# A decoder layer whose gate and up products become one group, with seven quarter products for eight in two of the eight pairs of k-blocks

## The chip, the cores and the metric

One core of one Trainium2 chip runs the whole layer. The metric is the time of one execution on the device, in microseconds. Engines: TensorE (PE: the matmuls; its weight loads, PEld, overlap them), VectorE (DVE), ScalarE (ACT), GpSimd (POOL, all but unused here) and SyncE (SP), whose queue issues nearly all DMA.

## What is computed

All arrays are float32, batch 1, 256 tokens, width 2048, feed-forward width 5632:

```python
def swiglu_half_ffn(x, norm_g, w_gate_up, w_down):
    h = rmsnorm(x, norm_g)
    gate, up = jnp.split(h @ w_gate_up, 2, axis=-1)
    return 0.5 * ((jax.nn.silu(gate) * up) @ w_down)

x = x + swiglu_half_ffn(x, ffn1_norm, ffn1_w_gate_up, ffn1_w_down)
# token mixers: h @ w_in, causal pooling, 16-head attention with forget gates,
# 4-head attention over 256 memory tokens, three sigmoid gates, merged @ w_out
x = x + merged @ w_out
x = x + swiglu_half_ffn(x, ffn2_norm, ffn2_w_gate_up, ffn2_w_down)
```

Each `w_gate_up` is 2048 x 11264 (gate columns first, then up columns) and each `w_down` is 5632 x 2048. The change is in the two feed-forward halves; the mixers between them are only renamed onto other buffers.

## The kernel before

**One product.** TensorE multiplies in a rounded form of float32 (float32r), so each operand is split into a high part and a low remainder, and a product takes three matmuls: high x high, high x low, low x high. `mm_group` (L208) makes 256 tokens x 512 columns: for each k-block of 128 rows and each of the two token blocks t, three matmuls of 128x128 weights (the activations, "lhs") against 128x512 streamed columns of the weight matrix. It streams the matrix through three `raw` buffers of 1 MB (four k-blocks by 512 columns, one DMA on SP's queue, L217). Each half of a `raw` buffer is cut into `wh` (ACT, L228) and `wl` (DVE, L229), which have three buffers each, and 12 matmuls (L235) use it. After each such half, `tick()` emits one piece of side work from the queue `side`; that is how transposes, head norms and attention run beside the large products.

**One feed-forward half** (`ffn`, L271) goes over 11 blocks c of 512 columns. For each it makes the gate product, then the up product (two groups of 96 matmuls), SiLU on ACT (L283), gate times up on DVE (L289), and appends two side steps that transpose the result (L188, four transposes each) and split it (ACT L177, DVE L178) into `hid`, which stays in SBUF. Then four column groups of `w_down`, each with 44 k-blocks (264 matmuls), go to the callback `cb`, which adds them to the stream `xs` and queues the transposes for the next norm (`residual`, L254).

**Buffers.** Large SBUF tiles come from one pool of 15 slabs of 8 KB per partition. PSUM has 8 banks: four (`mp`) for products and four (`ap`) for transposes and attention. The Tile framework fixes each engine's instruction order at build time; an engine executes its own list in order, and waits are semaphores.

Of the kernel before, what the change touches and what calls it, by code (L numbers as in the profile page):

```python
# [31 lines left out]
def hybrid_layer(  # L32
# [30 lines left out]
    sp = ctx.enter_context(tc.tile_pool(name="sp", bufs=15))  # L63
# [3 lines left out]
    mp = ctx.enter_context(tc.tile_pool(name="mp", bufs=4, space=PSUM))  # L67
    ap = ctx.enter_context(tc.tile_pool(name="ap", bufs=4, space=PSUM))
# [14 lines left out]
    def slab(shape, dtype, name):  # L83
        return sp.tile([P, *shape], dtype, tag="s", name=name)
# [4 lines left out]
    def aux(shape, name):  # L89
        return ap.tile([P, *shape], F32, tag="a", name=name)  # L90

# [66 lines left out]
    def rsqrt(ss, n, scale, name):  # L158
        """(ss * scale + EPS) ** -0.5 by Newton's iteration."""
# [23 lines left out]
    def to_lhs_part(dst, jj, src, gains, name):  # L183
# [5 lines left out]
        if gains is None or isinstance(gains, float):  # L189
            split(dst, 2 * jj, 2, ps, gains)  # L190
        else:
            for j in range(2):
                k = 2 * jj + j
                split(dst, k, 1, ps[:, j : j + 1, :], gains[:, k : k + 1])

    def to_lhs(tiles, src, gains, name):
        """Two steps that append [P, 4, 2, S], the parts of the transposes of src(t) [P tokens, 512], to tiles."""

        def first():
            tiles.append(slab([4, 2, S], F32R, name))  # L200
            to_lhs_part(tiles[-1], 0, src, gains, name)

        return [first, lambda: to_lhs_part(tiles[-1], 1, src, gains, name)]

    def lhs_of(tiles):
        return lambda k, part, t: tiles[k // 4][:, k % 4, part, t * P : (t + 1) * P]

    def mm_group(w, c0, kt, lhs, cols=((0, 512),), before=None):  # L208
# [3 lines left out]
        ps = [[mp.tile([P, 512], F32, tag="m", name="mm") for _ in cols] for _ in range(T)]  # L212
        cuts = [0, 1, 2, *range(4, kt + 1, per)] if before else [*range(0, kt, per), kt]
        for k0, k1 in zip(cuts, cuts[1:]):
# [6 lines left out]
            if before:  # L221
                before(k0)
            for h0 in range(0, nk, half):
                nh = min(half, nk - h0)
                wh = wp.tile([P, half, ncol], F32R, tag="wh", name="wh")
                wl = wp.tile([P, half, ncol], F32R, tag="wl", name="wl")
# [27 lines left out]
    def residual(gains, name):  # L254
        """Callback that adds a product to the stream and prepares the next norm."""
# [3 lines left out]
        def cb(c, ps):  # L259
# [9 lines left out]
        return cb, lhs_of(tiles), rs  # L269

    def ffn(lx, rs, wgu, wd, cb, before=None):  # L271
        hid = []
        rh = None
        for c in range(NFC):
            pg = mm_group(wgu, c * 512, KD, lx, before=before)
            before = None
            if c == 0:
                rh = st.tile([P, T], F32, tag="rh", name="rh")
                nc.vector.tensor_scalar(rh, rs[0], 0.5, None, ALU.mult)
            sg = []  # L280
            for t in range(T):
                s = temp([512], "sg")
                nc.scalar.activation(s, pg[t][0], AF.Silu, scale=rs[0][:, t : t + 1])  # L283
                sg.append(s)
            pu = mm_group(wgu, FF + c * 512, KD, lx)
            hd = []
            for t in range(T):
                h = temp([512], "hd")
                nc.vector.scalar_tensor_tensor(h, pu[t][0], rh[:, t : t + 1], sg[t], ALU.mult, ALU.mult)  # L289
                hd.append(h)  # L290
            side.extend(to_lhs(hid, lambda t, hd=hd: hd[t], None, "hid"))
        lh = lhs_of(hid)
        for c in range(4):
            cb(c, mm_group(wd, c * 512, KF, lh))

# [4 lines left out]
    def prepare(c, jj):  # L300
        cs = slice(c * 512, (c + 1) * 512)
        if jj == 0:
            tiles0.append(slab([4, 2, S], F32R, "x0"))
        to_lhs_part(tiles0[c], jj, lambda t: xs[:, t, cs], G_FFN1[:, 4 * c : 4 * c + 4], "x0")
# [26 lines left out]
    cb, lx, rs = residual(G_MIX, "x1")  # L331
    ffn(lhs_of(tiles0), rs0, ffn1_w_gate_up[0], ffn1_w_down[0], cb, before=before)

# [1 line left out]
    def head_norm(buf, nh, name):  # L335
        """buf [P, T, 1024 or 512]: each head over its own rms, in place."""
        hd = buf.shape[2] // nh
        hs = st.tile([P, T, nh], F32, tag=f"hs{nh}", name=name + "hs")
        for t in range(T):
            for c in range(buf.shape[2] // 512):  # L340
# [3 lines left out]
                nc.scalar.activation(sq, buf[:, t, cs].rearrange("p (h d) -> p h d", d=hd), AF.Square)  # L344
                nc.vector.tensor_reduce(hs[:, t, c * n : (c + 1) * n], sq, axis=AX.X, op=ALU.add)
        r = rsqrt(hs.rearrange("p t h -> p (t h)"), T * nh, 1.0 / hd, name)
        for t in range(T):
            b3 = buf[:, t, :].rearrange("p (h d) -> p h d", d=hd)
# [3 lines left out]
    def head_T(dst, buf, gain, scale, name):  # L352
        """Steps for dst [P, n, S] = transposes of buf [P, T, n*128], rows times gain and scale."""

        def step(jj):
            ps = aux([2, S], name)
            for j in range(2):
                for t in range(T):
                    k = 2 * jj + j
                    nc.tensor.transpose(ps[:, j, t * P : (t + 1) * P], buf[:, t, k * P : (k + 1) * P], ident)  # L360
            nc.vector.tensor_scalar(dst[:, 2 * jj : 2 * jj + 2, :], ps, gain, scale, ALU.mult, ALU.mult)

        return [lambda jj=jj: step(jj) for jj in range(buf.shape[2] // 256)]

    def project(w, c0, ncol, lhs, r, name):
        buf = slab([T, ncol], F32, name)
        for g in range(ncol // 512):
            ps = mm_group(w, c0 + g * 512, KD, lhs)
            for t in range(T):
                nc.scalar.activation(  # L370
                    buf[:, t, g * 512 : (g + 1) * 512], ps[t][0], AF.Copy, scale=r[0][:, t : t + 1]
# [8 lines left out]
    def load_mem():  # L380
        for t in range(T):
            mraw.append(slab([4, 512], F32, "mraw"))
            nc.sync.dma_start(
                out=mraw[t], in_=mem[0, t * P : (t + 1) * P, :].rearrange("p (c n) -> p c n", n=512)
            )
# [3 lines left out]
    for c in range(4):  # L389
        side.extend(to_lhs(mt, lambda t, c=c: mraw[t][:, c, :], G_MEM[:, 4 * c : 4 * c + 4], "memT"))  # L390
        side.append(lambda c=c: [sumsq(ssm, t, c, mraw[t][:, c, :]) for t in range(T)])
# [5 lines left out]
    qT = slab([8, S], F32, "qT")  # L397
# [4 lines left out]
    kT = slab([8, S], F32, "kT")  # L402
    side.extend(pause * 2 + head_T(kT, kf, G_FK, 1.0, "kT"))

# [4 lines left out]
    mqk = slab([2, 4, S], F32, "mqk")  # L409
    mqT, mkT = mqk[:, 0, :, :], mqk[:, 1, :, :]  # L410
    side.extend(pause * 4 + head_T(mkT, km, G_MK, 1.0, "mkT"))

# [1 line left out]
    ps = mm_group(win, 3584, KD, lx, cols=((0, 264), (264, 264)))  # L414
    z = st.tile([P, T, 16], F32, tag="z", name="z", bufs=1)
    qm = slab([T, 512], F32, "qm")
    for t in range(T):
        r = rs[0][:, t : t + 1]
        nc.vector.scalar_tensor_tensor(z[:, t, :], ps[t][0][:, :16], r, bforget, ALU.mult, ALU.add)
        nc.scalar.activation(qm[:, t, :248], ps[t][0][:, 16:264], AF.Copy, scale=r)  # L420
        nc.scalar.activation(qm[:, t, 248:], ps[t][1][:, :264], AF.Copy, scale=r)  # L421
# [3 lines left out]
    # log(1 + e) as log(u) + (e - (u - 1)) / u with u = 1 + e rounded  # L425
# [28 lines left out]
    def spread():  # L454
        for i in range(2):
            cb2.append(slab([8, S], F32, "cb"))
            nc.sync.dma_start(out=cb2[i], in_=cd[8 * i : 8 * i + 8, :].partition_broadcast(P))

    side.extend(pause * 2 + [cumulate])
    side.extend(head_T(mqT, qm, G_MQ, 1.0, "mqT"))  # L460
    side.append(spread)

# [4 lines left out]
    def staged(n, steps, gap):  # L467
        """Steps of n chains, each chain's first step ahead of the other steps of the chain before."""
# [11 lines left out]
    ym = slab([4, 2, S], F32R, "ym")  # L480
# [29 lines left out]
    def mem_values(h):  # L510
        ptc = mpt.pop(h)
        av = aux([S], "mav")
        for m in range(2):
            nc.tensor.matmul(av, vm[:, m, h * P : (h + 1) * P], ptc[:, m, :], start=m == 0, stop=m == 1)  # L514
        split(ym, h, 1, av.unsqueeze(1))
# [5 lines left out]
    ps = mm_group(win, 0, KD, lx)  # L521
    yp = slab([4, 2, S], F32R, "yp")
# [30 lines left out]
    def pool_mix(g):  # L553
        pm = aux([S], "pm")
        nc.tensor.matmul(pm, poolw[:, g, :], pooled.pop(g)[:, 16:], start=True, stop=True)
        split(yp, g, 1, pm.unsqueeze(1), G_POOL[:, g : g + 1])
# [14 lines left out]
    yf = [slab([4, 2, S], F32R, "yf") for _ in range(2)]  # L571
    fpr, fpt = {}, {}

    def fox_logits(pair):
# [3 lines left out]
        for lg, hs in halves:  # L578
            nc.tensor.matmul(lg[:, :P], qT[hs, pair, :P], kT[hs, pair, :P], start=True, stop=True)  # L579
        for lg, hs in halves:  # L580
            nc.tensor.matmul(lg[:, P:], qT[hs, pair, P:], kT[hs, pair, :], start=True, stop=True)  # L581
# [119 lines left out]
```

## Time and profile before

| | |
|---|---|
| median of three runs | 2194.72 us (2194.69 to 2194.9) |
| span of the profiled execution, first to last instruction | 2192.9 us |
| PE busy | 2184.6 us |
| DVE busy | 1158.2 us |
| ACT busy | 991.8 us |
| DMA moved | 413.10 MB, mean 188 GB/s |

The profiled execution's own time is known by its span; the runs are 1.8 us longer, which lies before the first and after the last instruction. The engines run beside each other, so busy times don't add up to the span. Matmuls overlap in the pipeline, so the duration of one matmul is longer than the step from one to the next.

### The profile page before, as it was taken

Reading aid. Unit: us, or ns where it says so; the run is one execution under the profiler, and the core shown is the slowest. Engines: PE = TensorE matmul, PEld = TensorE weight load, DVE = VectorE, ACT = ScalarE, POOL = GpSimd, SP = SyncE. Lnnn points to the kernel's source line nnn. Section 1 sums busy time; section 2 is a strip of 40 time slices with the busy share of each in tenths; the row PEclk is TensorE's granted clock in tenths of the full one; section 3 lists DMA queues with packets and bytes.
Section 4 is the critical chain, followed back from the end, with each engine's and each line's share of the span. In section 5 each row is a group of like instructions: output and inputs, shape, how many; then the busy total and the mean of one; then the engine's idle time right before and its main releaser. Section 6 shows DMA issues by size and latency. Waiting matters only on the chain.

```text
span 2192.9 us, 24640 instructions
## 1 busy us (share of the span) xinstructions
PE 2184.6 (100%) x9986; PEld 1803.2 (82%) x9986; DVE 1158.2 (53%) x1335; ACT 991.8 (45%) x1192; POOL 3.5 (0%) x24
## 2 busy tenths in 40 slices
PE   9999999999999999999999999999999999999999
PEld 7888888888888888887788888888888888888887
DVE  5544454444445576657555555554455445544444
ACT  5444444444444554556544444444444444443333
POOL 0000000000000000000000000000000000000000
PEclk9999999999999999999999999999999999999999
DMA  7555555555555654654466655555555555556664
GB/s 243 188 185 191 192 192 189 187 189 189 188 192 191 230 173 156 238 171 136 137 195 195 195 182 190 191 185 189 189 189 189 192 192 192 183 188 205 204 199 134
DMA packets 206870, 413.10 MB, mean 188 GB/s; under 512 B 6734, under 2 KB 7844, under 8 KB 206244
## 3 DMA queue, kind: packets, MB, share of 16 engines
q1 hardware_dynamic: 206464, 411.48, 57.0%
q8 instruction: 78, 1.28, 0.2%
q14 instruction: 36, 0.29, 0.0%
q10 hardware_dynamic: 292, 0.05, 0.0%
HBM read 409.38 MB, written 2.11 MB: 188 GB/s over the span
## 4 chain that ended last, share of the span: by engine, by line
PE 99%; DMA 1%; ACT 0%; DVE 0%; SPq 0%; issue 0%; ACTq 0%
PE mm L235 95%; PE hid L188 1%; DMA raw<-in_ffn_w_gate_up_dram 1%; PE x L188 0%; PE fpt L609 0%; PE fav L619 0%; PE flg L581 0%; PE flg L579 0%; PE memT L188 0%; PE mg L188 0%; PE mlg L487 0%; PE mav L514 0%; PE fav L621 0%; PE fav L620 0%; ACT wh L228 0%; PE mpt L506 0%
## 5 line engine op out<-in xcount | busy, mean ns | idle before, releaser
L229 DVE TENSOR_TENSOR wl<-raw,wh 128x1024 fp32r<-128x1024 f32 (+2 forms) x777 | 942.3, 1213 | 970.9 <-ACT wh L228 970.4
L228 ACT ACTIVATE wh<-raw 128x1024 fp32r<-128x1024 f32 (+2 forms) x777 | 815.6, 1050 | 1114.4 <-PE mm L235 1094.5
L235 PE MATMUL mm<-wh,x 128*128 128x512 f32 (+1 forms) x4160 | 1286.8, 388 | 0.6 <-ACT x L180 0.6
L235 PEld LDWEIGHTS mm<-wh,x 128*128 128x128 f32 x4160 | 776.3, 188 | 159.4 <-issue 1.8
L235 PE MATMUL mm<-wl,x 128*128 128x512 f32 (+1 forms) x2080 | 804.3, 387 | 0.5 <-DVE wl L229 0.5
L235 PEld LDWEIGHTS mm<-wl,x 128*128 128x128 f32 x2080 | 390.7, 188 | 78.3 <-issue 1.2
L235 PE MATMUL mm<-wh,hid 128*128 128x512 f32 x1408 | 435.9, 390 | 0.0
L235 PEld LDWEIGHTS mm<-wh,hid 128*128 128x128 f32 x1408 | 264.3, 188 | 54.9
L235 PE MATMUL mm<-wl,hid 128*128 128x512 f32 x704 | 273.9, 389 | 0.0
L235 PEld LDWEIGHTS mm<-wl,hid 128*128 128x128 f32 x704 | 132.2, 188 | 27.1
L235 PE MATMUL mm<-wh,mg 128*128 128x512 f32 x256 | 80.4, 392 | 0.0
L235 PEld LDWEIGHTS mm<-wh,mg 128*128 128x128 f32 x256 | 48.1, 188 | 9.9
L235 PE MATMUL mm<-wl,mg 128*128 128x512 f32 x128 | 49.9, 390 | 0.0
L235 PE MATMUL mm<-wh,memT 128*128 128x512 f32 x128 | 40.6, 393 | 0.1
L235 PE MATMUL mm<-wh,yf 128*128 128x512 f32 x128 | 40.0, 389 | 0.0
L180 ACT ACTIVATE x<-x,cols 128x256 fp32r<-128x256 f32 x48 | 20.8, 474 | 25.5 <-PE x L188 15.5
L289 DVE SCALAR_TENSOR_TENSOR hd<-mm,rh,sg 128x512 f32<-128x512 f32 x44 | 30.9, 743 | 0.0
L235 PEld LDWEIGHTS mm<-wh,memT 128*128 128x128 f32 x128 | 24.0, 188 | 5.2 <-ACT qm L421 0.3
L178 DVE TENSOR_TENSOR hid<-hid 128x512 fp32r<-128x512 f32 x44 | 28.2, 682 | 0.0
L235 PEld LDWEIGHTS mm<-wh,yf 128*128 128x128 f32 x128 | 24.0, 188 | 5.0
L235 PEld LDWEIGHTS mm<-wl,mg 128*128 128x128 f32 x128 | 24.1, 188 | 4.7
L181 DVE SCALAR_TENSOR_TENSOR x<-x,cols,x 128x256 fp32r<-128x256 f32 x48 | 21.6, 479 | 10.2 <-ACT x L180 10.0
(226 smaller groups left out, 724.1 us busy)
## 6 DMA issues: line engine op xcount, KB each, us to landing
raw<-in_ffn_w_gate_up_dram SPq DMA_DIRECT2D x175, 1024.0 KB, 5.0
raw<-in_ffn_w_down_dram SPq DMA_DIRECT2D x88, 1024.0 KB, 5.1
raw<-in_w_in_dram SPq DMA_DIRECT2D x76, 1024.0 KB, 5.1
raw<-in_w_out_dram SPq DMA_DIRECT2D x16, 1024.0 KB, 5.1
raw<-in_w_mem_kv_dram SPq DMA_DIRECT2D x8, 1024.0 KB, 5.9
raw<-in_w_fox_o_dram SPq DMA_DIRECT2D x8, 1024.0 KB, 5.3
raw<-in_w_pool_up_dram SPq DMA_DIRECT2D x4, 1024.0 KB, 5.1
raw<-in_w_mem_o_dram SPq DMA_DIRECT2D x4, 1024.0 KB, 5.1
```

Of the source, the lines that this page charges most:

```text
L178: nc.vector.tensor_tensor(lo, src, h.bitcast(F32), ALU.subtract)
L180: nc.scalar.activation(h, src, AF.Copy, scale=gain)
L181: nc.vector.scalar_tensor_tensor(lo, src, gain, h.bitcast(F32), ALU.mult, ALU.subtract)
L188: nc.tensor.transpose(ps[:, j, t * P : (t + 1) * P], src(t)[:, k * P : (k + 1) * P], ident)
L228: nc.scalar.activation(hv, rv, AF.Copy)
L229: nc.vector.tensor_tensor(lv, rv, hv.bitcast(F32), ALU.subtract)
L235: nc.tensor.matmul(ps[t][i][:, :n], lhs(k, part, t), wt[:, kk, o : o + n], start=k == 0 and q == 0, stop=k == kt - 1 and q == 2,)
L289: nc.vector.scalar_tensor_tensor(h, pu[t][0], rh[:, t : t + 1], sg[t], ALU.mult, ALU.mult)
```

## The change

For blocks c = 1 to 10 of each feed-forward half, gate and up columns are made by one `pair_group`. It goes over eight pairs u of k-blocks in the order 2, 0, 3, 1, 4, 5, 6, 7; a pair's `raw` buffer holds two k-blocks of gate columns and the same two of up columns (two DMAs of 512 KB). Six pairs are multiplied plainly. In pairs 0 and 1 the 2x2 arrangement (two token blocks, two k-blocks) x (two k-blocks, gate and up columns) is done with seven products in place of eight (a form of Strassen's identity with shared sums, after Winograd). The sums of activations are made once for each half by `form_page`, those of the weights in each block by DVE. Three of the products accumulate straight into results, four into banks of their own (p1, p5, p6, p7), which DVE combines into four terms after pair 1; these are added to the four results at the group's end. Side work runs only in the last four pairs.

The middle of the feed-forward half (blocks 0 to 9, transposed but not split) is stored to DRAM, and is loaded and split during the first column group of `w_down`. Slabs of 8 KB become 26 pages of 4 KB, `wh`/`wl` get five buffers each, and all eight PSUM banks form one pool. The other edits replace slabs by pages (two or four tiles for one) and drop comments.

```diff
-    sp = ctx.enter_context(tc.tile_pool(name="sp", bufs=15))
+    pp = ctx.enter_context(tc.tile_pool(name="pg", bufs=26))
...
-    mp = ctx.enter_context(tc.tile_pool(name="mp", bufs=4, space=PSUM))
-    ap = ctx.enter_context(tc.tile_pool(name="ap", bufs=4, space=PSUM))
+    mp = ctx.enter_context(tc.tile_pool(name="mp", bufs=8, space=PSUM))
...
+    def form_page(forms, tiles, j):
+        xp = tiles[j]
+        v, f = temp([2, S], "fv"), temp([4, P], "ff")
+        nc.vector.tensor_tensor(v, xp[:, :, 0, :].bitcast(F32), xp[:, :, 1, :].bitcast(F32), ALU.add)
+        a12, a22, a11, a21 = (v[:, kk, t * P : (t + 1) * P] for kk in range(2) for t in range(T))
+        nc.vector.tensor_tensor(f[:, 0, :], a21, a22, ALU.subtract)
+        nc.vector.tensor_tensor(f[:, 1, :], f[:, 0, :], a11, ALU.subtract)
+        nc.vector.tensor_tensor(f[:, 2, :], a11, a21, ALU.subtract)
+        nc.vector.tensor_tensor(f[:, 3, :], f[:, 1, :], a12, ALU.add)
+        dst = page([2, 4, P], F32R, "form")
+        nc.scalar.activation(dst[:, 0, :, :], f, AF.Copy)
+        nc.vector.tensor_tensor(dst[:, 1, :, :], f, dst[:, 0, :, :].bitcast(F32), ALU.subtract)
+        forms.append(dst)
+    def parts(n):
+        return (
+            wp.tile([P, n], F32R, tag="wh", name="wh", bufs=5),
+            wp.tile([P, n], F32R, tag="wl", name="wl", bufs=5),
+        )
+    def cut(dst, src):
+        nc.scalar.activation(dst[0], src, AF.Copy)
+        nc.vector.tensor_tensor(dst[1], src, dst[0].bitcast(F32), ALU.subtract)
+    def add_product(ps, sides, wt, col, start, stop):
+        for q, (part, i) in enumerate(((0, 0), (1, 0), (0, 1))):
+            nc.tensor.matmul(
+                ps, sides[part], wt[i][:, col : col + 512], start=start and q == 0, stop=stop and q == 2
+            )
+    def pair_group(w, c0, c1, lhs, forms, order):
...
+        for i, u in enumerate(order):
+            end = i == len(order) - 1
+            raw = wp.tile([P, 2, 2, 512], F32, tag="raw", name="raw")
+            for n, cc in enumerate((c0, c1)):
+                nc.sync.dma_start(
+                    out=raw[:, n, :, :],
+                    in_=w[2 * u * P : (2 * u + 2) * P, cc : cc + 512].rearrange("(k p) c -> p k c", p=P),
+                )
+            if u not in seven:
+                for n in range(2):
+                    wt = parts(1024)
+                    cut(wt, raw[:, n, :, :].rearrange("p k c -> p (k c)"))
+                    for t in range(T):
+                        for kk in range(2):
+                            ps, start, stop = into((t, n), end and kk == 1)
+                            add_product(ps, [lhs(2 * u + kk, q, t) for q in range(2)], wt, kk * 512, start, stop)
+                    if i > order.index(seven[-1]) if seven else True:
+                        tick()
+                continue
+            last = u == seven[-1]
+            s = raw.rearrange("p n k c -> p (n k) c")
+            plain = parts(1024)
+            cut(plain, s[:, 0:2, :].rearrange("p s c -> p (s c)"))
+            ta, tb = page([2, 512], F32, "ta"), page([2, 512], F32, "tb")
+            nc.vector.tensor_tensor(ta, s[:, 3:4, :].to_broadcast([P, 2, 512]), s[:, 1:3, :], ALU.add)
+            ha = (page([1024], F32R, "hah"), page([1024], F32R, "hal"))
+            cut(ha, ta.rearrange("p s c -> p (s c)"))
+            plain2 = parts(512)
+            cut(plain2, s[:, 2, :])
+            nc.vector.tensor_tensor(tb[:, 0, :], ta[:, 0, :], s[:, 2, :], ALU.add)
+            nc.vector.tensor_tensor(tb[:, 1, :], tb[:, 0, :], s[:, 0, :], ALU.add)
+            hb = (page([1024], F32R, "hbh"), page([1024], F32R, "hbl"))
+            cut(hb, tb.rearrange("p s c -> p (s c)"))
...
+            for key, sides, wt, col in (
+                ("p1", xq(1, 0), plain, 512),
+                ((0, 0), xq(0, 0), plain, 0),
+                ("p5", fm(0), ha, 0),
+                ("p7", fm(2), ha, 512),
+                ((0, 1), fm(3), plain2, 0),
+                ("p6", fm(1), hb, 0),
+                ((1, 0), xq(0, 1), hb, 512),
+            ):
+                ps, start, stop = into(key, last if isinstance(key, str) else end)
+                add_product(ps, sides, wt, col, start, stop)
+            if last:
+                a, u3, u4, v = (temp([512], n) for n in ("ua", "u3", "u4", "uv"))
+                nc.scalar.activation(a, acc["p1"], AF.Copy)
+                nc.vector.tensor_tensor(u3, acc["p6"], a, ALU.add)
+                nc.vector.tensor_tensor(u4, acc["p5"], u3, ALU.subtract)
+                nc.vector.tensor_tensor(u3, acc["p7"], u3, ALU.add)
+                nc.vector.tensor_tensor(v, acc["p5"], u3, ALU.subtract)
+                terms = {(0, 0): a, (1, 0): u3, (0, 1): u4, (1, 1): v}
+        return acc, terms
...
+            if c == 2:
+                side.extendleft(pause * 3)
             if c == 3:
                 rs.append(row_rstd(ss, name))
...
+        def put(c, hd):
...
+                nc.scalar.activation(dst[0][:, 2 * jj : 2 * jj + 2, :], ps, AF.Copy)
+                if jj == 1:
+                    nc.sync.dma_start(out=hdram[c], in_=dst[0].rearrange("p k s -> p (k s)"))
+        def get(c):
+            if c < NFC - 1:
+                flat[c] = page([4, S], F32, "hg")
+                nc.sync.dma_start(out=flat[c].rearrange("p k s -> p (k s)"), in_=hdram[c])
+        def use(c):
+            if c < NFC - 1:
+                f = flat.pop(c)
+                for jj in range(2):
+                    hid.append(page([2, 2, S], F32R, "hid"))
+                    split(hid[-1], 0, 2, f[:, 2 * jj : 2 * jj + 2, :])
...
+        for c in range(1, NFC):
+            if c == NFC - 1:
+                side.extend(put_last)
+            acc, terms = pair_group(wgu, c * 512, FF + c * 512, lx, forms, (2, 0, 3, 1, 4, 5, 6, 7))
+            for n in range(2):
+                for t in range(T):
+                    d = terms[t, n]
+                    nc.vector.tensor_tensor(d, acc[t, n], d, ALU.add)
+            hd = gated(c, [terms[t, 0] for t in range(T)], [terms[t, 1] for t in range(T)])
+            if c < NFC - 1:
+                side.extend(put(c, hd))
+            if c == NFC - 2:
+                put_last = [lambda: get(0), lambda: get(1)]
...
+        def need(k0):
+            c = k0 // 4
+            if c + 2 < NFC - 1:
+                get(c + 2)
+            if c + 1 < NFC - 1:
+                use(c + 1)
```

## Rows read from the trace of the kernel before

**Rows 1.** The page's first part and the head of its second: busy time, share of the span and instructions of each engine; then the span in 40 slices, busy share in tenths.

```profile
span 2192.9 us, 24640 instructions
PE 2184.6 (100%) x9986; PEld 1803.2 (82%) x9986; DVE 1158.2 (53%) x1335; ACT 991.8 (45%) x1192; POOL 3.5 (0%) x24
PE   9999999999999999999999999999999999999999
PEclk9999999999999999999999999999999999999999
DMA  7555555555555654654466655555555555556664
```

**Rows 2.** The chain of work that ended last: its share of the span by engine, and two neighbouring pieces of gate and up and two of `w_down` (start us, us, what).

```profile
PE 99%; DMA 1%; ACT 0%; DVE 0%; SPq 0%; issue 0%; ACTq 0%
330.29 42.88 PE mm L235 x189
374.74 42.88 PE mm L235 x189
...
508.08 59.20 PE mm L235 x261
568.85 59.20 PE mm L235 x261
```

**Rows 3.** Busy time of each engine in the first and the last stretch of the span.

```profile
0.00:50.00 50.00, 45.71 (x199) 34.82 (x200) 26.92 (x49) 29.74 (x53) 2.25 (x12) 1.00 0.75 249
2180.00:2193.00 13.00, 9.02 (x40) 7.13 (x38) 3.10 (x4) 1.06 (x1) 0.00 (x0) 1.00 0.10 40
```

**Rows 4.** Groups of instructions on DVE, shapes kept apart: line, operation, shapes, count, busy us, mean ns of one, idle before.

```profile
L229 DVE TENSOR_TENSOR wl<-raw,wh 128x1024 fp32r<-128x1024 f32 x759 | 929.6, 1225 | 959.6 <-ACT wh L228 959.3
L289 DVE SCALAR_TENSOR_TENSOR hd<-mm,rh,sg 128x512 f32<-128x512 f32 x44 | 30.9, 743 | 0.0
L178 DVE TENSOR_TENSOR hid<-hid 128x512 fp32r<-128x512 f32 x44 | 28.2, 682 | 0.0
L651 DVE TENSOR_TENSOR acc<-acc,gate 128x512 f32<-128x512 f32 x16 | 10.3, 680 | 0.0
L650 DVE TENSOR_TENSOR gate<-mm,gate 128x512 f32<-128x512 f32 x16 | 10.2, 681 | 0.0
L350 DVE TENSOR_TENSOR qf<-qf,qfy 128x1024 f32<-128x1024 f32 x2 | 2.4, 1222 | 0.0
L543 DVE TENSOR_TENSOR pool<-pool 128x256 f32<-128x256 f32 x10 | 4.2, 424 | 0.6
L229 DVE TENSOR_TENSOR wl<-raw,wh 128x512 fp32r<-128x512 f32 x2 | 1.4, 692 | 3.4 <-ACT wh L228 3.3
```

**Rows 5.** The same for ACT, and one `wh` of 512 columns from the timeline (start us, us).

```profile
L228 ACT ACTIVATE wh<-raw 128x1024 fp32r<-128x1024 f32 x759 | 804.2, 1060 | 1096.2 <-PE mm L235 1079.3 <-issue 10.4 <-DVE nm L594 3.2
L177 ACT ACTIVATE hid<-hid 128x512 fp32r<-128x512 f32 x44 | 23.5, 586 | 0.0
L283 ACT ACTIVATE sg<-mm,x0y 128x512 f32<-128x512 f32 x22 | 15.1, 689 | 9.7 <-PE mm L235 9.7
...
5.00 0.63 ACT L228 ACTIVATE wh<-raw 128x512 fp32r<-128x512 f32 x1 [2.22 <-DMA raw<-in_ffn_w_gate_up_dram]
```

**Rows 6.** Who waited for whom (us in total, times, longest us), and the same for SP's queue.

```profile
ACT wh L228 <- PE mm L235: 1094.5, 678, 3.9
DVE wl L229 <- ACT wh L228: 970.4, 723, 3.3
PE x L188 <- DMA xs<-in_x_dram: 1.8, 2, 1.5
PE mm L235 <- ACT x L180: 0.6, 1, 0.6
...
SPq L217 <- DVE wl L229: 1799.1, 352, 9.2
SPq L457 <- DMA cd<-ncT: 3.4, 1, 3.4
SPq L447 <- DVE ncT L446: 1.1, 1, 1.1
```

**Rows 7.** DVE's and ACT's timeline over the end of one block's up group (start us, us, in brackets the idle time before).

```profile
366.82 1.23 DVE L229 TENSOR_TENSOR wl<-raw,wh 128x1024 fp32r<-128x1024 f32 x1 [1.49 <-ACT wh L228]
367.96 1.41 DVE L289 SCALAR_TENSOR_TENSOR hd<-mm,rh,sg 128x512 f32<-128x512 f32 x2
369.54 1.23 DVE L229 TENSOR_TENSOR wl<-raw,wh 128x1024 fp32r<-128x1024 f32 x1 [0.18 <-ACT wh L228]
372.26 1.22 DVE L229 TENSOR_TENSOR wl<-raw,wh 128x1024 fp32r<-128x1024 f32 x1 [1.49 <-ACT wh L228]
...
368.45 1.06 ACT L228 ACTIVATE wh<-raw 128x1024 fp32r<-128x1024 f32 x1 [1.66 <-PE mm L235]
371.17 1.06 ACT L228 ACTIVATE wh<-raw 128x1024 fp32r<-128x1024 f32 x1 [1.66 <-PE mm L235]
```

**Rows 8.** DMA issues: count, KB each, median us from issue to landing; and the length of one issue on SP's queue (ns, min/median/max).

```profile
raw<-in_ffn_w_gate_up_dram SPq DMA_DIRECT2D x175, 1024.0 KB, 5.0
cb<-cd SPq DMA_DIRECT2D x2, 1024.0 KB, 4.3
out_dram<-o SPq DMA_DIRECT2D x8, 256.0 KB, 6.7
raw<-in_ffn_w_gate_up_dram SPq DMA_DIRECT2D x1, 512.0 KB, 5.9
...
L217 SPq DMA_DIRECT2D raw<-in_ffn_w_gate_up_dram x178: 367/368/470, 1.3 to 1926.6; - x178
```

More of the change, by code (lines that the diff above doesn't have):

```diff
@@ L81, in drain, with page, pages, bank @@
             tick()
-    def slab(shape, dtype, name):
-        return sp.tile([P, *shape], dtype, tag="s", name=name)
+    def page(shape, dtype, name):
+        return pp.tile([P, *shape], dtype, tag="p", name=name)
+    def pages(n, shape, dtype, name):
+        return [page(shape, dtype, name) for _ in range(n)]
+    def bank(name):
+        return mp.tile([P, 512], F32, tag="m", name=name)
     def temp(shape, name, dtype=F32):
@@ L193, in to_lhs_part @@
                 k = 2 * jj + j
-                split(dst, k, 1, ps[:, j : j + 1, :], gains[:, k : k + 1])
+                split(dst, j, 1, ps[:, j : j + 1, :], gains[:, k : k + 1])
     def to_lhs(tiles, src, gains, name):
[L199 to L203, printed above, removed]
+        return [lambda jj=jj: to_lhs_part(tiles, jj, src, gains, name) for jj in range(2)]
@@ new lines, in pair_group, with into @@
+    def pair_group(w, c0, c1, lhs, forms, order):
+        seven = [u for u in order if u < len(forms)]
+        acc = {}
+        sums = {}
+        terms = []
+        kinds = [(0, 0), (1, 0), (0, 1), (1, 1)]
+        def into(key, last):
+            if key not in acc:
+                acc[key] = bank("mm")
+                return acc[key], True, last
+            return acc[key], False, last
+        for i, u in enumerate(order):
[31 more added lines that the diff above has]
+            cut(hb, tb.rearrange("p s c -> p (s c)"))
+            fm = lambda m: [forms[u][:, q, m, :] for q in range(2)]
+            xq = lambda kk, t: [lhs(2 * u + kk, q, t) for q in range(2)]
+            for key, sides, wt, col in (
[18 more added lines that the diff above has]
+        return acc, terms
@@ L210, in mm_group @@
+    def mm_group(w, c0, kt, lhs, cols=((0, 512),), before=None, need=None):
         ncol = sum(n for _, n in cols)
         per, half = 2048 // ncol, 1024 // ncol
-        ps = [[mp.tile([P, 512], F32, tag="m", name="mm") for _ in cols] for _ in range(T)]
+        ps = [[bank("mm") for _ in cols] for _ in range(T)]
         cuts = [0, 1, 2, *range(4, kt + 1, per)] if before else [*range(0, kt, per), kt]
@@ L265, in cb @@
                 sumsq(ss, t, c, xs[:, t, cs])
+            if c == 2:
+                side.extendleft(pause * 3)
             if c == 3:
                 rs.append(row_rstd(ss, name))
[L269 to L285, printed above, removed]
+        return cb, tiles, rs
@@ new lines, in ffn, with turn, gated @@
+    def ffn(lx, xt, rs, wgu, wd, cb, before=None):
+        hid, forms, flat = [], [], {}
+        hdram = dp.tile([NFC - 1, P, 4 * S], F32, tag="hd", name="hd", bufs=2)
+        rh = st.tile([P, T], F32, tag="rh", name="rh")
+        def put(c, hd):
+            dst = []
+            def turn(jj):
+                if jj == 0:
+                    dst.append(page([4, S], F32, "hf"))
+                ps = aux([2, S], "hid")
+                for j in range(2):
+                    for t in range(T):
+                        k = 2 * jj + j
+                        nc.tensor.transpose(ps[:, j, t * P : (t + 1) * P], hd[t][:, k * P : (k + 1) * P], ident)
+                nc.scalar.activation(dst[0][:, 2 * jj : 2 * jj + 2, :], ps, AF.Copy)
+                if jj == 1:
+                    nc.sync.dma_start(out=hdram[c], in_=dst[0].rearrange("p k s -> p (k s)"))
+            return [lambda: turn(0), lambda: turn(1)]
+        def get(c):
[8 more added lines that the diff above has]
+                    split(hid[-1], 0, 2, f[:, 2 * jj : 2 * jj + 2, :])
+        def gated(c, gate, up):
@@ L292, in ffn @@
+        drain()
+        use(0)
+        last = to_lhs(hid, lambda t: hd[t], None, "hid")
+        def need(k0):
[4 more added lines that the diff above has]
+                use(c + 1)
+            elif c + 1 == NFC - 1:
+                for f in last:
+                    f()
         lh = lhs_of(hid)
         for c in range(4):
-            cb(c, mm_group(wd, c * 512, KF, lh))
+            cb(c, mm_group(wd, c * 512, KF, lh, need=need if c == 0 else None))
@@ L381, in load_mem @@
         for t in range(T):
[L382 to L385, printed above, removed]
+            mraw.append(pages(2, [2, 512], F32, "mraw"))
+            for i in range(2):
+                nc.sync.dma_start(
+                    out=mraw[t][i],
+                    in_=mem[0, t * P : (t + 1) * P, i * 1024 : (i + 1) * 1024].rearrange("p (c n) -> p c n", n=512),
+                )
     side.append(load_mem)
@@ L568, in hybrid_layer @@
     drain()
-    yf = [slab([4, 2, S], F32R, "yf") for _ in range(2)]
+    yf = pages(4, [2, 2, S], F32R, "yf")
     fpr, fpt = {}, {}
```

134 lines of the change are left out of this document (77 added, 57 removed).

## The prediction

> **What bounds the kernel now.** I read the page's busy times first: PE is busy 2184.6 of 2192.9 us and at full granted clock in every slice, DVE for 53%, ACT for 45%, the DMA engines for about 57% [rows 1]. Busy alone would not prove a limit, since matmuls overlap, so I read the chain of waits next: PE owns 99% of it, in nearly unbroken pieces [rows 2]. The two pairs of pieces give the price of a matmul. One block of gate and up takes 374.74 - 330.29 = 44.45 us for 192 matmuls and 8 transposes; one group of `w_down` takes 568.85 - 508.08 = 60.77 us for 264 and 8. The difference is 72 matmuls in 16.32 us: 0.2267 us each, and then 0.116 us for a transpose (44.45 - 43.52 = 0.93 us for eight). PE stands idle for some 8 us in all, 4.3 us of it in the first 50 us and 4.0 us in the last 13 [rows 3]; between those it waits for others hardly at all, at most 0.6 us for the operands of products [rows 6]. DVE and ACT do wait, and in a ring: ACT for PE (1094.5 us: a `wh` buffer comes free), DVE for ACT (970.4 us), SP for DVE (1799.1 us) [rows 6]. So PE sets the pace, and a matmul that goes away gives back its 0.2267 us unless something else ends last.
>
> **What the change removes.** A plain pair of k-blocks costs 2 x 2 x 2 x 3 = 24 matmuls, one with quarter products 7 x 3 = 21. Two such pairs in each of 10 blocks in each of two halves: 2 x 3 x 20 = 120 matmuls, 120 x 0.2267 = **27.2 us**, or 1.36 us a block. Transposes are as many as before. The new group is 186 x 0.2267 + 0.93 = 43.09 us of PE. By the Trainium skill, "TensorE: Matmul & The Clock Gate", section "Wait — 56ns, not 53.3ns?", a warm 512-column matmul would step every 215.7 ns, which would make the saving 25.9 us. The chain shows the longer step over whole blocks, and I use that.
>
> **What it adds on DVE and ACT.** Before, a block costs DVE 16 x 1.225 + 2 x 0.743 + 2 x 0.682 = 22.45 us [rows 4]. After: six plain pairs 12 x 1.225 = 14.70; a pair with quarter products three remainders of 1024 (1.225), one of 512 (0.692), a sum of 1024 (`ta`, priced like the 1.222 us of L350) and two of 512 (`tb`, 0.680 each): 6.95, twice 13.90; four terms and four final adds at 0.681, 5.45; gate times up 1.49. Sum 35.5 us in 43.09: 82% busy. Over 20 blocks that is some 289 us more in total (14.45 a block with the hidden middle's split, which moves to `w_down`). ACT goes from 16 x 1.060 + 2 x 0.689 + 2 x 0.586 = 19.5 us to 18 x 1.060 + 2 x 0.63 + 0.586 + 1.38 + 1.17 = 23.5 us, 54% [rows 5], and 1.17 us a block in `w_down` for the split moved there. Both stay below PE on the mean, but not evenly. From the start of a group to the terms, DVE has 4.90 + 13.90 + 2.72 and, from the group before, 2.72 + 1.49: 25.7 us, against 90 matmuls or 20.4 us of PE. It falls 5.3 us behind there and gets it back in the last four pairs (9.80 us of work in 22.7).
>
> Is there a lead of 5.3 us? With five buffers, a part is cut four parts ahead of its use, 4 x 2.72 = 10.9 us, less the 1.06 + 1.23 us that the cut takes [rows 7]: 8.6 us. The shared sums and their remainders (5.0 us a pair) don't go through those buffers; they need only the raw data and pages. With three raw buffers, pair 0's data is asked for when pair 6 is cut, about 17 us before the group starts, and lands 5 us later; so its 5.0 us of sums fit into some 18 us before PE reaches p5. Pair 1's data waits for pair 2's cut, lands about 2 us into the group, and its sums are due at 17 us; with pair 3, the plain parts of pairs 0 and 1 and pair 4's first cut, DVE has about 12 us to do in those 15. It fits with a few microseconds to spare. Lower end: no stall. Upper end: DVE runs each pair's steps strictly in turn and sits through every ACT copy (3 x 1.060 + 0.63 = 3.8 us a pair); then its first half is 33.4 us, 4.4 us more than 20.4 + 8.6, in each of 20 groups: 88 us. I take zero, because the trace shows the instruction order interleaving such work (gate times up slips between two remainders with 0.18 us of idle time behind it [rows 7]).
>
> **The banks.** A group uses four banks for results and four for p1, p5, p6, p7, so all eight are taken from pair 0 to the terms; before, a product group took two of eight. The four of the p's are free again after pair 1, the side transposes borrow two at a time in the last four pairs, and the next group's first pair needs four. They are free when it starts, and the old results' four are added away by DVE (2.7 us) before pair 0's p1 wants one, 5.4 us later. Cost zero; if a borrowed bank or a late add stands in the way, 0.68 us a group for each add waited for.
>
> **Stores, loads and SP's queue.** Twenty stores and twenty loads of 512 KB add 21 MB to 413 at about 57% DMA use. A store is issued on SP's queue behind the ACT copy that makes its data, and raw loads stand behind it. Before, `cd`'s store held that queue for 1.1 us and the load that needs it for 3.4 us [rows 6]. A raw load lands 5.0 us after issue [rows 8] and its buffer comes round every three pairs, 16 us, so some 10 us are spare; that covers such a wait, and the second 0.37 us issue per pair too. The new late point is the start of `w_down`: block 0's load is ticked some 13.6 us (five half pairs) before the last group ends; a load of 5.9 us [rows 8] and two splits (2 x 1.27) take 8.4 us. Should it also wait for block 9's store to land (6.7 us is the nearest row, a smaller store), it is 1.5 us late, twice: 0 to 3 us. In the first group of `w_down`, DVE gets 2 x 1.225 + 2 x 0.682 = 3.8 us for each 5.44 us of PE. `form_page` costs DVE about 0.68 + 0.69 + 4 sums of 128 columns (0 to 0.42 each): at most 3.1 us a page beside block 0, covered by the 22 us that DVE idles there (44.45 - 22.45). The three pauses before the third transposes leave them to the middle of the last `w_down` group, after four pages of `hid` are used up; hidden. For all of these I take 1 us.
>
> **Sum.** 2192.9 - 27.2 + 1.0 = 2166.7 us of span, and 1.8 us around it: **2168.5 us**.
>
> **Rivals.** (a) *Bank hand-over.* PE waits at each group's start for one or two final adds on DVE, 0.68 to 1.36 us x 20: 2181 to 2195 us. For it: all eight banks are in one pool, and the side transposes take some just then. Against: the four p banks come free three pairs earlier. (b) *DVE becomes the bound*, the side of a slower kernel: in the first four pairs of each group PE waits for hb of pair 1 or pair 0, up to 4.4 us a group, 2167.5 + 88 = 2255 us. It decides from 1.36 us a group on, where the saving is gone. For it: DVE is 5.3 us behind PE there and each sum must go DVE, ACT, DVE. Against: the lead worked out above and 18% of idle time. (c) *The clock.* Rows 1 show 1.00 granted, 2.4 GHz, throughout. If hand-overs of banks made PE pause often enough that half a pair (2.72 us) per group ran at 1.2 GHz, that is 2.72 x 20 = 54 us, 2222 us. By the Trainium skill's same page, section "A second HAM failure mode: psum-queue depth-cycling", a kernel that cycles through its PSUM banks can lose the clock that way; the trace before, which rotates four banks without a pause, shows none of it. (d) *The change frees no time*, because another engine ended the blocks before: the chain speaks against it.
>
> **Numbers.** Forecast, with its bounds 2166 to 2174 us: 0.66. Smaller stalls up to rival (a)'s: 0.18, of which 0.03 end within 0.2% of before. DVE as the bound: 0.12, of which 0.01 within 0.2%. Clock 0.03, no effect 0.01. A change of 0.2% (4.4 us) is about what a measurement of this kernel can tell from none: faster 0.81, within 0.2% 0.05, slower 0.14. The range goes from 2165.5, a microsecond or two under the sum, into rival (a): to 2187.
>
> **What would show it.** Right: 9866 PE instructions, PE still near 100% busy, blocks stepping every 43.1 us in the chain, `w_down` groups at 60.8 us, DVE near 1450 us and ACT near 1095 us busy, clock 1.00, and no wait of PE of more than a few microseconds in total. Wrong: gaps of PE before p5, p6 or the first pair, released by DVE (b) or by the final adds (a); a slice of clock under full; or SP waiting on a store while ACT waits for `raw`.

## The result, and the profile after

The changed kernel takes 2163.81 us (2163.19 to 2164.44) against 2194.79: ratio 0.9857, 95% interval 0.9844 to 0.9871, 31 us faster. The forecast was 2168.5 with a range from 2165.5: the direction was right, but the gain was larger than the range allowed. The profiled execution took 2164.44 us with a span of 2162.7.

The page's first two parts, which answer to [rows 1]:

```profile
span 2162.7 us, 25374 instructions
PE 2153.8 (100%) x9866; PEld 1779.2 (82%) x9866; DVE 1417.4 (66%) x1719; ACT 1082.6 (50%) x1336; POOL 3.5 (0%) x24
PEclk9999999999999999999999999999999999999999
```

PE has the 120 instructions less and is still the engine that is always busy, at full clock; DVE has gone from 53% to 66%. The chain of waits, for [rows 2] (start us, us, what): two neighbouring blocks of gate and up, and one group of `w_down`.

```profile
300.65 39.47 PE mm L240 x174
343.77 39.47 PE mm L240 x174
...
556.56 59.20 PE mm L345 x261
617.33 65.30 PE mm L345 x288
```

A block steps in 343.77 - 300.65 = 43.12 us (forecast 43.09) where it took 44.45, and a group of `w_down` still in 60.77. The waits, for [rows 6]:

```profile
ACT wh L234 <- PE mm L240: 196.8, 150, 3.8
...
SPq L403 <- ACT hf L401: 43.1, 20, 7.9
```

No row has PE waiting for a sum (`ta`, `tb`), a term or a bank in the new groups (L240). SP's queue waits 2.2 us on the mean for each store to DRAM, and no wait of PE follows from it.

So where do the missing 4.0 us of span lie (2166.7 forecast, 2162.7 measured)? Two rows for each kernel mark the stages: the start of the last matmul of the first feed-forward half (second number after "ns") and of the last of `w_out`. Before, then after:

```profile
L235 PE MATMUL mm<-wh,hid x704: 389/389/485, 501.6 to 744.4; 128*128 128x512 f32 x176
L235 PE MATMUL mm<-wh,mg x256: 389/389/478, 1369.0 to 1459.5; 128*128 128x512 f32 x128
```

```profile
L345 PE MATMUL mm<-wh,hid x704: 389/389/478, 489.3 to 732.2; 128*128 128x512 f32 x176
L345 PE MATMUL mm<-wh,mg x256: 389/389/484, 1352.1 to 1442.6; 128*128 128x512 f32 x128
```

The first half ends 12.2 us earlier, the second, to the span's end, takes 720.1 instead of 733.4, 13.3 us less: together 25.5 of the 27.2 us that the removed matmuls are worth. The mixers between, which I had taken for the same work under other buffer names, fell from 715.1 to 710.4 us: **4.7 us that no term of the sum has.** PE is 100% busy there in both kernels, because the matmuls' reported durations overlap; only the order on PE shows it. The chain over one pair of heads of the forgetting attention, from one head's attention-times-values (`fav`) to the next pair's, before (the view leaves out its shortest pieces, so read the times from start to start):

```profile
1043.20 0.36 PE fav L619 x2
1044.00 0.66 PE mm L235 x2
1044.66 0.42 PE flg L579 x4
1045.09 0.36 PE fav L619 x2
1045.45 0.22 PE fav L620 x2
1045.88 0.63 PE flg L581 x4
1046.52 2.99 PE mm L235 x12
1049.51 0.33 PE fpt L609 x3
1049.84 1.40 PE mm L235 x6
1051.23 0.33 PE fpt L609 x3
1051.56 3.66 PE mm L235 x16
1055.21 0.36 PE fav L619 x2
```

After:

```profile
1028.72 0.36 PE fav L800 x2
...
1029.58 0.22 PE fav L802 x2
1029.80 0.43 PE mm L345
1030.23 0.42 PE flg L760 x4
1030.65 0.43 PE flg L762 x4
1031.08 2.95 PE mm L345 x12
1034.03 0.66 PE fpt L790 x6
1034.69 5.27 PE mm L345 x23
1039.95 0.36 PE fav L800 x2
```

The same matmuls (36 large ones) take 12.0 us before and 11.2 after. Before, the two heads' `fav` are 0.80 us each and stand apart, with large matmuls and logits (`flg`) between; after, both take 1.08 us as one piece, and the logits and the transposes (`fpt`) are whole too. Over the eight pairs of heads, the chain has the two heads' `fav` together in two pairs before and in six after. The first and last `fav` (first of three lines of each kernel's view), before, after, and in the first run below, which has only the shared banks:

```profile
L619 PE MATMUL fav<-fptc,vf x32: 272/298/324, 1008.8 to 1088.1; 128*64 128x128 f32 x32
L800 PE MATMUL fav<-fptc,vf x32: 272/298/324, 994.9 to 1070.9; 128*64 128x128 f32 x32
L618 PE MATMUL fav<-fptc,vf x32: 272/298/324, 1008.6 to 1084.6; 128*64 128x128 f32 x32
```

From the first to the last it is 79.3 us before and 76.0 after: 3.3 of the 4.7 us. Another 1.7 us lie between the first half's end and the first `fav` (264.4 us before, 262.7 after), which the torn pieces of attention's values don't explain; 0.3 us is lost again behind the last.

### The profile page after: what moved, and what is told of

It is laid out like the page before. It is cut to its first block, busy times and chain, and to the rows that moved or that the text cites. A ratio compares the mean times of both kernels' runs of the same rounds, so it can differ in the third digit from the quotient of the medians.

```text
span 2162.7 us, 25374 instructions
## 1 busy us (share of the span) xinstructions
PE 2153.8 (100%) x9866; PEld 1779.2 (82%) x9866; DVE 1417.4 (66%) x1719; ACT 1082.6 (50%) x1336; POOL 3.5 (0%) x24
## 4 chain that ended last, share of the span: by engine, by line
PE 99%; DMA 1%; DVE 0%; ACT 0%; SPq 0%; ACTq 0%; issue 0%
PE mm L345 57%; PE mm L240 39%; PE hid L400 1%; DMA raw<-in_ffn_w_gate_up_dram 1%; PE x L196 0%; PE fpt L790 0%; PE fav L800 0%; PE mg L196 0%; PE memT L196 0%; PE flg L762 0%; PE mlg L668 0%; PE mav L695 0%; PE flg L760 0%; PE fav L802 0%; PE fav L801 0%; PE qT L533 0%
## 5 line engine op out<-in xcount | busy, mean ns | idle before, releaser
L339 DVE TENSOR_TENSOR wl<-raw,wh 128x1024 fp32r<-128x1024 f32 (+2 forms) x457 | 549.6, 1204 | 498.6 <-ACT wh L338 497.8
L338 ACT ACTIVATE wh<-raw 128x1024 fp32r<-128x1024 f32 (+2 forms) x457 | 475.9, 1044 | 580.7 <-PE mm L345 559.2
L240 PE MATMUL mm<-wh,x 128*128 128x512 f32 x2080 | 644.0, 391 | 0.0
L234 ACT ACTIVATE wh<-raw 128x1024 fp32r<-128x1024 f32 x320 | 321.4, 1005 | 349.7 <-PE mm L240 196.8
L345 PE MATMUL mm<-wh,x 128*128 128x512 f32 (+1 forms) x1600 | 492.1, 385 | 2.3 <-ACT x L185 2.3
L240 PEld LDWEIGHTS mm<-wh,x 128*128 128x128 f32 x2080 | 388.0, 188 | 79.2
L235 DVE TENSOR_TENSOR wl<-raw,wh 128x1024 fp32r<-128x1024 f32 x320 | 367.0, 1154 | 118.7 <-ACT wh L234 118.4
L240 PE MATMUL mm<-wl,x 128*128 128x512 f32 x1040 | 403.4, 390 | 0.0
L345 PEld LDWEIGHTS mm<-wh,x 128*128 128x128 f32 x1600 | 296.1, 188 | 62.0 <-ACT x L185 3.0
L345 PEld LDWEIGHTS mm<-wh,hid 128*128 128x128 f32 x1408 | 264.4, 188 | 54.6
L345 PE MATMUL mm<-wl,x 128*128 128x512 f32 (+1 forms) x800 | 306.4, 383 | 0.0
L240 PEld LDWEIGHTS mm<-wl,x 128*128 128x128 f32 x1040 | 195.3, 188 | 41.0
L345 PEld LDWEIGHTS mm<-wl,hid 128*128 128x128 f32 x704 | 132.2, 188 | 27.3
L285 DVE TENSOR_TENSOR ta<-raw 128x1024 f32<-128x1024 f32 x40 | 49.0, 1225 | 50.7 <-DMA raw<-in_ffn_w_gate_up_dram 50.7
L234 ACT ACTIVATE hah<-ta 128x1024 fp32r<-128x1024 f32 x40 | 42.3, 1058 | 25.5 <-DVE ta L285 25.2
```

The lines of the kernel that those rows point to most:

```text
L234: nc.scalar.activation(dst[0], src, AF.Copy)
L235: nc.vector.tensor_tensor(dst[1], src, dst[0].bitcast(F32), ALU.subtract)
L240: nc.tensor.matmul(ps, sides[part], wt[i][:, col : col + 512], start=start and q == 0, stop=stop and q == 2)
L285: nc.vector.tensor_tensor(ta, s[:, 3:4, :].to_broadcast([P, 2, 512]), s[:, 1:3, :], ALU.add)
L338: nc.scalar.activation(hv, rv, AF.Copy)
L339: nc.vector.tensor_tensor(lv, rv, hv.bitcast(F32), ALU.subtract)
```

## The experiments

All are compared with the kernel before in runs of the same chip (2194.7 to 2195.0 us). "Mixers" is the time between the two marks above.

**Shared banks alone**, on the kernel before:

```diff
-    mp = ctx.enter_context(tc.tile_pool(name="mp", bufs=4, space=PSUM))
-    ap = ctx.enter_context(tc.tile_pool(name="ap", bufs=4, space=PSUM))
+    mp = ctx.enter_context(tc.tile_pool(name="mp", bufs=8, space=PSUM))
...
-        return ap.tile([P, *shape], F32, tag="a", name=name)
+        return mp.tile([P, *shape], F32, tag="m", name=name)
```

> The kernel before with one edit: its two PSUM pools of four banks become one pool of eight. Theory 1 (the shared banks let both heads' small matmuls of the forgetting attention stand next to each other in PE's order): the attention stretch shrinks as in the changed kernel, one pair of heads beside the value and gate products from 12.0 to about 11.2 us, and the time falls by 4 to 5 us, to about 2190 us; the blocks of gate and up stay at 44.45 us. Theory 2 (the gain in the mixers comes from five buffers for wh and wl, or from the smaller pages): 2194.8 us, within 1 us.

2191.5 us (ratio 0.9984, 0.9975 to 0.9993), blocks still 44.45 us. Its mark of `w_out`:

```profile
L234 PE MATMUL mm<-wh,mg x256: 389/389/477, 1365.8 to 1456.2; 128*128 128x512 f32 x128
```

With the first half's end at 744.5, the mixers take 711.7 us: 3.4 of the 4.7 us. From the first to the last `fav` it is 76.0 us, as in the changed kernel; six of the eight pairs stand together, and one of those is down to 11.2 us (`fav` at 1042.41 and 1053.65 us in its chain). Theory 1 holds, a little short of its 4 to 5 us.

**Eight products in all pairs**, the rest of the change kept:

```diff
-        for j in range(2):
-            form_page(forms, xt, j)
...
-                    d = terms[t, n]
-                    nc.vector.tensor_tensor(d, acc[t, n], d, ALU.add)
+                    terms[t, n] = acc[t, n]
```

> The changed kernel with eight products in all eight pairs: no sums of activations or weights, no terms; the one group for gate and up, the middle in DRAM, pages, five buffers and shared banks stay. If the quarter products are worth what their matmuls are (1.32 us a block by the two traces, 20 blocks) and the rest of the change gives the gain in the mixers: 2163.8 + 26.4 = 2190.2 us, blocks back at about 44.45 us, mixers as short as in the changed kernel. If the grouping itself gave part of the blocks' gain, it is below 2189 us; if the round trip through DRAM costs PE time in this form, above 2192 us.

2191.07 us (0.9982, 0.9973 to 0.9991): the quarter products are worth 2191.07 - 2163.81 = 27.3 us, beside 27.2 for 120 matmuls at 0.2267 us (26.7 by the two profiled spans). The mixers take 710.4 us, as in the changed kernel. Grouping, the middle in DRAM and the pages cost PE some 1.2 us: blocks step 44.51 us (110.25 and 154.75 us in the chain are two starts) where they took 44.45, twenty times.

**Four and four banks in the mixers**, the rest of the change kept:

```diff
+    part_banks()
...
+    share()
```

(the pool of eight is closed after the first half, two pools of four are opened, and back before the second).

> The changed kernel with two pools of four banks between the two feed-forward halves, as the kernel before has them; the halves keep the one pool of eight. Theory 1 (shared banks): the mixers lose their gain, 2163.8 + 4.5 = 2168.3 us, with the attention's small matmuls split up again; up to 2 us more where the pools change over. Theory 2 (buffers or pages): 2163.8 us, within 1 us.

2170.4 us, 6.6 us more than the changed kernel; mixers 715.4 us, and 79.4 us from the first `fav` to the last, both as before the change. PE waits 2.0 us where the pools change over; of the two waits (us, times, longest) only the first, 0.98 us at 733.30, lies in the mixers:

```profile
PE mm L357 <- DVE xs L384: 2.0, 2, 1.0
```

Without it the mixers would be some 0.7 us shorter than before. So without the shared banks five buffers for `wh` and `wl` give the mixers about that much, and nothing between the first `fav` and the last.

**Three buffers for `wh` and `wl`** instead of five:

```diff
-            wp.tile([P, n], F32R, tag="wh", name="wh", bufs=5),
-            wp.tile([P, n], F32R, tag="wl", name="wl", bufs=5),
+            wp.tile([P, n], F32R, tag="wh", name="wh", bufs=3),
+            wp.tile([P, n], F32R, tag="wl", name="wl", bufs=3),
```

> The changed kernel with three buffers for wh and wl in place of five. By the prediction's account of the lead, a part is then cut only two parts ahead (5.4 us less 2.3 us for the cut: 3.1 us) while DVE falls 5.3 us behind PE in the first four pairs: about 2.2 us of waiting in each of 20 groups, 2163.8 + 44 = 2208 us, PE waiting for wl or the sums in the first half of each group. Rival: the shared sums do not pass through these buffers and DVE does them early, so the time stays within 3 us of 2163.8. If the buffers gave the gain in the mixers, 2168 us with blocks still at 43.13 us.

2168.03 us, 4.2 us more, and not 44. Two neighbouring blocks in its chain:

```profile
1690.71 40.18 PE mm L240 x177
1733.83 40.18 PE mm L240 x177
```

Blocks stay at 43.12 us. The mixers take 711.7, as with shared banks and three buffers above: the five buffers are the other 1.3 us of the mixers. They lie ahead of the first `fav` (263.9 us from the first half's end, 262.7 with five buffers); what is shorter there stays open. The remaining 3 us lie in the two halves, outside the steady blocks: PE waits 0.9 us for ACT's `wh` near the start of each, and the rest is not assigned. So my account of DVE's lead, which rested on five buffers, was wrong, and the rival expectation right in its reason, if not within its 3 us: the sums don't pass through those buffers. The third expectation's 2168 us is met by luck, since only 1.3 of the 4.2 us are in the mixers.

**Attention's values side by side**, on the kernel before, banks and buffers untouched: in `fox_values` the six matmuls of a pair are emitted head by head in turn and pinned together.

```diff
-        for i, ptc in enumerate(fpt.pop(pair)):
...
+        ptcs = fpt.pop(pair)
+        for step in range(3):
+            for i in (1, 0):
...
+                if not first:
+                    tc.keep_in_program_order(m)
```

> The kernel before, banks and buffers untouched, with one edit: the six matmuls of attention weights times values of a pair of heads are pinned next to each other, the two heads in turn. Theory 1a (the gain in the mixers is that small matmuls of two heads, which use different halves of the array, run beside each other when they stand together; 1.08 us in place of 2 x 0.80 us per pair): 8 x 0.5 = 4 us less, 2190.9 us, at the old banks. Theory 1b (the gain is fewer turns between small and large matmuls of every kind, or waits for banks): under 1.5 us less, 2193.5 to 2195 us. If pinning makes PE wait for the second head, slower.

2187.41 us (0.9966, 0.9954 to 0.9979): 7.4 us less, more than either theory gave. One pair of heads in its chain:

```profile
1033.03 0.81 PE fav L627 x12
1033.83 0.42 PE flg L579 x4
1034.25 0.43 PE flg L581 x4
...
1045.33 0.81 PE fav L627 x12
```

Two heads take 0.81 us, what one took before: they run beside each other. It is not only that one head's weight loads hide behind the other's matmuls: `mlg`, the logits of the memory attention, in the same float32 but over all 128 rows and columns, takes 0.86 us in the chain before for four matmuls of 256 columns, so 0.108 us for 128 columns, and the twelve of 128 columns take 0.067 each:

```profile
908.72 0.86 PE mlg L487 x4
```

By the Trainium skill, "TensorE: Matmul & The Clock Gate", section "Part 3: Packing small matmuls — row/col tiling", matmuls that fill only some columns of the array can run concurrently in different column tiles; a head's values fill 64 of 128, and this trace agrees, 0.81 against 2 x 0.80 us. All eight pairs take 0.81 to 0.83 us; before, six took 1.60 and two 1.08, so this is 6 x 0.79 + 2 x 0.27 = 5.3 of the 7.4 us. For the other 2.1 there are pieces that were not asked to stand together but now do (the second `flg` takes 0.43 us in place of 0.63), and fewer turns between small and large matmuls; these were not separated.

**The same pinning on the changed kernel.**

> The changed kernel with the same pinning. Two or three of its eight pairs of heads still have the two heads' matmuls apart: about 0.5 us each, 2162.5 us. If theory 1b holds, 2163.8 us, within 0.5 us.

2161.07 us, 2.7 us less, and mixers of 707.9 us against 707.4 with the old banks. With the order pinned, the mixers are about as long with the old banks and three buffers as with the new ones (707.9 has one wait of PE in it, 1.7 us for a `fav` operand): what the banks had given was the order.

**Quarter products in three pairs.**

```diff
-        for j in range(2):
+        for j in range(3):
...
-            acc, terms = pair_group(wgu, c * 512, FF + c * 512, lx, forms, (2, 0, 3, 1, 4, 5, 6, 7))
+            acc, terms = pair_group(wgu, c * 512, FF + c * 512, lx, forms, (3, 0, 4, 1, 5, 2, 6, 7))
```

> The changed kernel with quarter products in three pairs (0, 1 and 2; order 3, 0, 4, 1, 5, 2, 6, 7). DVE gets 4.5 us more per block, 40 of 42.4 us. If matmuls still set the pace, each block loses three more of them and the further 0.02 us or so: 2163.8 - 13.4 = 2150.4 us, blocks at about 42.45 us. If DVE now ends last (the rival of the prediction), PE waits for the sums of pairs 1 and 2 and the time lies between 2150 and well over 2164 us; every us of waiting per block costs 20 us.

2153.18 us (0.9809, 0.9796 to 0.9823), blocks at 42.45 us as worked out; 2.8 us of the expected gain are lost outside the steady blocks. PE waits 2.9 us for `hbh`, a copy of the shared sums, once in the first group of each half (1.4 us each), a wait that the changed kernel doesn't have: the sums first end last there. DVE is busy 187.6 of 212.2 us over five blocks, 88%.

**The same with the sums on GpSimd** (`ta` and `tb` by `nc.gpsimd.tensor_tensor`).

> The same three pairs, with the sums of weights (ta, tb) on GpSimd in place of DVE, which takes 2.6 us per pair from DVE. If DVE was short of time with three pairs, this gives it back: 2150.4 us. If GpSimd and DVE hinder each other when both read SBUF, DVE's instructions of 1.225 us grow longer in the trace and the time is above that of three pairs on DVE. If DVE was never short, the same time as three pairs on DVE, within 1 us.

2166.77 us, 13.6 us more than with the sums on DVE. Groups of instructions, first a sum on GpSimd, then two of DVE's remainders:

```profile
L285 POOL TENSOR_TENSOR ta<-raw 128x1024 f32<-128x1024 f32 x60 | 158.0, 2633 | 1006.0 <-DMA raw<-in_ffn_w_gate_up_dram 898.2 <-DVE u L312 37.8 <-DVE wl L235 31.2
...
L235 DVE TENSOR_TENSOR hal<-ta,hah 128x1024 fp32r<-128x1024 f32 x60 | 82.3, 1372 | 65.8 <-ACT hah L234 65.8
L235 DVE TENSOR_TENSOR wl<-raw,wh 128x512 fp32r<-128x512 f32 x60 | 55.7, 928 | 2.1 <-ACT wh L234 2.1
```

The remainders that took 1.22 and 0.68 us with the sums on DVE take 1.37 and 0.93 us: the two engines hinder each other. That the 13.6 us are this alone is not shown. From 230 us on, blocks step 42.45 us here too; 7.1 us are lost in the first half, before that, and the chain there also passes through GpSimd's own `ta` (pieces of 3.17 and 5.12 us).

**Quarter products in four pairs** (order 4, 0, 1, 5, 2, 3, 6, 7).

> The changed kernel with quarter products in four pairs (0 to 3; order 4, 0, 1, 5, 2, 3, 6, 7). In the traces DVE is busy 33.5 us of a 43.13 us block with two pairs and 37.5 of 42.44 with three, so four ask about 41.5 us of DVE for a block of 180 matmuls, 41.8 us. If the matmuls alone set the pace: 41.8 us a block and 2137 us. The prediction's rival, DVE as the bound, should show here: no idle time left to wait for ACT's copies, PE waiting for the sums in every block, blocks of 42.5 to 44.5 us, 2150 to 2190 us, so no better than three pairs.

2262.69 us, slower than the kernel before (1.0312, 1.0295 to 1.0329) and than I expected. Its chain, in one block:

```profile
342.63 0.44 PE hid L400 x4
...
356.41 1.22 DVE ta L285
357.63 1.15 DVE wl L235
358.79 3.60 DMA raw<-in_ffn_w_gate_up_dram
362.49 1.07 ACT wh L234
...
390.80 0.44 PE hid L400 x4
```

This block takes 390.80 - 342.63 = 48.2 us (its neighbours 44 to 48) where its matmuls need 41.8. DVE is busy 41.3 us of it, which would just fit; what ends last in this block is a ring: `raw` is held until DVE's last instruction that reads it, only then does the next load start, and its 3.6 us and the following cut come on top. With two pairs, three `raw` buffers had hidden that. Over the whole run PE's waits end in nearly equal parts at copies of `raw` (`wh`) and of the shared sums (`hbh`), and they cost clock as well (us waited, times, longest; then each engine's busy time and the granted clock, 0.96, in the block shown):

```profile
PE mm L240 <- ACT wh L234: 36.1, 36, 2.8
PE mm L240 <- ACT hbh L234: 34.4, 22, 1.9
...
342.63:390.80 48.17, 44.15 (x190) 35.14 (x189) 41.30 (x47) 25.53 (x29) 0.00 (x0) 0.96 0.55 190
```

PE stood idle for 2.35 us up to 380.50, and from 380 to 384 us the granted clock was 0.58: for most of that time 1.2 in place of 2.4 GHz. Over the block PE is idle 4.0 us, and 4% of clock is by estimate 1.9 us more: together most of the 6.4 us above 41.8. Over the run the mean granted clock is 0.99, which by the same estimate is some 23 us; each of the four executions shows it (0.989 to 0.991), while the changed kernel's show 1.00.

**Three pairs and the pinning together.**

> The changed kernel with quarter products in three pairs and the attention's small matmuls pinned together. The two gains lie in different stretches and both have PE as the bound, so they should add: 2153.2 - 2.7 = 2150.5 us, blocks at 42.44 us, mixers as long as with the pinning alone.

2151.96 us (0.9806, 0.9791 to 0.9820), the fastest of all: 11.9 us under the changed kernel. The mixers take 707.9 us as they should; 1.5 us are lost in the feed-forward halves, where PE waits 1.8 us for `hbh` near the start of each.

## Why the prediction was right and wrong

- *The price of a matmul* was right: 27.3 us by the control with eight products, 27.2 in the sum. By the step of the Trainium skill, "TensorE: Matmul & The Clock Gate", section "Wait — 56ns, not 53.3ns?", it would by estimate have been 25.9 us; the runs stand with the chain, 27.3.
- *Stalls of 1 us* were 1.7: 0.03 us a block, and 0.9 us in the first 20 us, where PE is busy 14.8 us instead of 15.7. There PE waits for the second load of weights, which landed at 15.92 us instead of 15.00 (lines below). In seven other runs built on the changed kernel it landed between 14.4 and 15.7 us, so this is put down to the one profiled execution, the slowest of four, and not to the change.
- *DVE and ACT hidden* was right, 33.5 us of DVE a block against 35.5 worked out: consecutive instructions of 1.225 us start 1.14 us apart. Its reason was half wrong: the lead does not hang on five buffers (blocks of 43.12 us with three, and a wait of 0.9 us once in each half).
- *The banks at zero* is the step that failed. I asked only what eight shared banks might cost the new groups; I did not ask what they do to the mixers, which I had taken as only renamed. They gave 3.4 us there by themselves, because attention's small matmuls were less often torn apart in the order on PE; the five buffers, which the sum also had at nothing for the mixers, gave the other 1.3 us of the 4.7, by a way that stays open. With 4.7 us more the sum is 2162.0 us of span, 0.7 from the measured. The row that could have said it was in the trace before: one head's `fav`, `flg` and the other's `fav` as separate pieces of the chain, under 100% busy.
- *Rivals.* Banks cost nothing and the clock stayed at 1.00 although all eight banks are cycled. DVE's side as the bound was a real mechanism with the wrong point: with three pairs it costs 2.9 us in the first groups, and it decides with four, where loads wait for DVE, PE waits for the copies, and the pauses bring the clock rival with them (0.99 over the run).

The second load of weights (start us, us), before, then after:

```profile
6.50 8.50 DMA raw<-in_ffn_w_gate_up_dram
6.89 9.03 DMA raw<-in_ffn_w_gate_up_dram
```

That bank shortage is what tore the pieces apart is inferred: the order on PE changed with the banks, and pinning the order gave the same without them. Which wait of the build-time ordering did it stays open.

## What to carry to other kernels

A change of buffers also changes the order in which other stages are laid out, so cost every stage that shares a pool, also those that the change does not name. On a busy PE look for torn pieces in the chain: 100% busy hides that two half-width matmul groups could stand together. When an engine gets more work, follow the buffer that it holds: with four pairs, in the block followed, it was late loads, with DVE just short of full, and the pauses then cost clock too.

## What the runs showed of the hardware

- Two heads' matmuls of 64 columns, next to each other, took 0.81 us for twelve, as long as six of one head alone. The second logits of two heads, 64 rows each, took 0.43 us for four of 256 columns, where four over the whole array (`mlg`) took 0.86.
- With four pairs, where PE paused for up to 2.8 us at a time, the granted clock fell to 0.58 over one stretch of 4 us and to 0.99 over the run.
- GpSimd took 2.63 us for a sum of 1024 columns that DVE does in 1.22, and lengthened DVE's own two-input instructions beside it by 12 to 36% (1.22 to 1.37, 0.68 to 0.93 us). By the Trainium skill, "SBUF — State Buffer", section "Who interferes with whom", a VectorE instruction with two inputs in SBUF contends with a GpSimd instruction that reads SBUF, because its second input comes through a read interface that they share; the lengthened rows agree.
